# Recurrent gates on four 64x64 tiles, GpSimd subtractions in pieces, and a reordered prelude

## The chip, the cores and the metric

The kernel runs on one core of one Trainium2 chip. The core has TensorE (PE; PEld is its weight load), VectorE (DVE), ScalarE (ACT), GpSimd (POOL) and SyncE (SP), which issues nearly all DMAs from one queue in program order. The metric is the device time of one execution in microseconds. The kernel before took 1122.44 us (median of 3 runs, 1121.16 to 1125.28).

## The reference

One layer over 256 latent tokens and 256 context tokens, D = 1024, all in float32. Cut to its steps:

```python
mod = silu(c) @ w_ada + b_ada                     # 6 x 1024, also for c_ctx
zl  = modulate(rms_norm(x),   sh1, sc1) @ w_in    # 2048 columns
zc  = modulate(rms_norm(ctx), csh1, csc1) @ w_in  # only the recurrent columns count
conv_l = conformer_conv(zl[:, :512], zl[:, 512:1024])      # GLU, 31 taps, layer norm, silu
ul, uc = dwconv(zl[:, 1024:1536]), dwconv(zc[:, 1024:1536]) # 4 taps
for d in (forward, backward):                     # two directions
    r = sigmoid(u @ wa[d, head] + ba[d])          # 8 heads of 64 x 64
    i = sigmoid(u @ wx[d, head] + bx[d])
    a = exp(-8 r softplus(-lam[d]));  b = sqrt(1 - a^2) i u
    h += scan(a, b, start = end of the context's scan)
lru_l = h * gelu(zl[:, 1536:])
x = x + g1 * (concat(conv_l, lru_l) @ w_out)
h2 = modulate(rms_norm(x), sh2, sc2)
x = x + g2 * moe(h2)          # 32 experts of 1024 x 1024 x 3 weights, 2 per token
out = rms_norm(x)
```

## The kernel before

The **prelude** is everything ahead of the experts. Its weights (w_ada, w_in, w_out) pass through 17 slots of 128x2048 float32, the activations of the two token sets lie side by side as 512 columns. The **experts** follow one after another: each reads 12.6 MB of weights into nine 128x4096 buffers, wide0 to wide8, which lie on the memory of the prelude's slots and are used in the order of WORDER. So a weight load of the first round waits on SyncE's queue until the last prelude step that uses the memory under its buffer is done, and all later loads stand behind it. After expert 1 VectorE computes the largest expert load; SyncE reads it into a register (line 1038) ahead of the next loads on its queue.

**Split products.** Some float32 products are made from three fp32r passes. For that a weight is split: `split_hi` makes a rounded high half (HI, ZH, WH, MH name the engine by letters V, S, G), and `split_lo` (line 303) subtracts it to make the low half (LO, ZL, WL, ML). A slot has 2048 columns, so each is one instruction of 128x2048. `load_wz` and ZL do this for the four quarters of w_in's convolution columns, with `prepare` (lines 292 to 294) making the modulated inputs for `vgproj` (line 331); o0 and o1 do it for the recurrent columns u (used by `u_mm`, line 377), J4 for one part of w_out (used by `oproj`, line 680).

**Order.** From the end of the third quarter on, the prelude runs by the words of ORDER, a list written out by hand. Each word appends one step to the queues of its engines, which run in that order. The words that matter here: v vgproj, h and o the halves of u, l GLU, t a convolution tap on VectorE, s a side tap (scaled on ScalarE, added on GpSimd), i the same scaled on VectorE, u and c the recurrent projection and its 4 taps, p gate matmuls (`gate_mm`, line 397), a gate activations (`gate_act`, lines 407 to 414), d, q and n the recurrence, b one of 16 ada steps with its load (lines 505 to 511), z and e the gelu branch, M, C, Q, R and N the layer norm, I, J and X the splits for w_out, O the output projection, D, Y, H and K the second norm and router matmuls, T, P, F and A the selection, G and U the first gather, W idle matmuls (`warm`). With OS = "0010" only I4, J4, X4 and X5 do anything among the I, J and X words.

**Gates.** A gate step makes two banks, pa for r and pi for i. Each bank has the two heads of a 128-channel tile as 64x64 matmuls at tile positions (0, 0) and (64, 64). A float32 matmul stands in the trace as two records. `gate_act` takes three activations from pa, a square, and one tanh of pi with the halved biases hb (line 225).

Of the kernel before, what the change touches and what calls it, by code (L numbers as in the profile page):

```python
# [7 lines left out]
F32 = mybir.dt.float32  # L8
# [3 lines left out]
AF = mybir.ActivationFunctionType  # L12
OP = mybir.AluOpType
# [8 lines left out]
SLOTS = 17  # L22
WIDE = 9

WORDER = (0, 7, 5, 2, 1, 6, 4, 3, 8)


SP = 384
# [2 lines left out]


ORDER = """
v0 h0 o0 l0 v2 t v3 t h1 v1 t o1 u0 t*4 l2 u1 l1 t b t s b s t*2 s*2 t s t*2 s*2 t i t*2 s t l3 s*2 i t s t*4 s b t*2
s t c1 t*2 s*3 t s*2 t*2 s*2 t s i t c0 b*2 s u2 s*2 t p10 c2 s t s t p11 t s p00 b s a10 t a00 t i*2 u3 w b t*2 p20 t
i t*2 p01 s*2 c3 t p30 s*2 t*2 s t d10 s*2 i p21 t a20 s*2 t*2 d00 t a30 t d30 s t b t b z0 t s t a01 r1 d20 s q10 s*2
t*2 b t*2 s L0 t*2 s q20 t*4 L4 z1 I0 s q30 t p31 q00 t n00 t*2 n20 s b d01 a11 M b a31 k1 C2 z2 C1 a21 n10 C0 L2 d11
C3 d21 q11 b q21 q01 d31 z3 Q n01 b R e0 N1 N2 X1 N0 I2 L6 x b X2 N3 X0 n30 J2 J0 O001 e3 q31 O112 I4 e2 X3 n11 I6
O012 O111 O010 J4 b e1 O002 O100 O011 O110 g O113 n31 O102 n21 m1 X5 j J6 m3 O101 O000 O003 X7 O103 m0 O005 O017 O007
O013 r2 m2 X6 k2 X4 O006 O105 O104 O004 O015 O114 O014 D00 O107 O016 O115 D01 H00 O106 Y0 D10 O117 O116 H01 H10 y D11  # L40
K00 H11 K01 K10 Z0 T0 K11 P0 F0 G06 B G04 G02 Y1 T1 G07 G05 P1 Z1 G03 G00 F1 A1 G01 G10 G11 G12 U0 G16 G17 G14 G15 U4
U1 G13 U2 U3 U6 U5 U7 A0
"""
VTAPS = (31, 0, 9, 31)

PC = (0, 3)
SIDE = (1, 2,)
HI, LO = "SS", "GG"
SQ = ("SGGG", "SSSS")
LNSQ = "SGSG"  # L50
XC = ("VS", "SV")
WH, WL = "SSVV", "VVGV"
MH, ML = "GGGGGSSG", "GVGVGVGG"
GL = ("GG", "GG")
OS = "0010"
ZH, ZL = "SSSS", "GGGG"
FN = "VS"


COLS = {}  # L60
# [9 lines left out]
def hybrid_layer(ctx: ExitStack, tc: tile.TileContext, sp_d, x_d, c_d, bada_d, rb_d, fg_d, gw_d,  # L70
                 wada_d, win_d, wout_d, w1_d, w3_d, w2_d, out_d):
    nc = tc.nc
    V, S, G, P = nc.vector, nc.scalar, nc.gpsimd, nc.tensor
    dma = nc.sync.dma_start

    const = ctx.enter_context(tc.tile_pool(name="const", bufs=1))
# [33 lines left out]
    def col(name, i=None, n=1):  # L110
        a, b = COLS[name]
        return sp[:, a:b] if i is None else sp[:, a + i:a + i + n]
# [110 lines left out]
    V.tensor_scalar(nkh, kh, -1.0, None, OP.mult)  # L223
    hb = sp[:, COLS["ba"][0]:COLS["bx"][1]]
    V.tensor_scalar(hb, hb, 0.5, None, OP.mult)
    dwh = col("dw")
    V.tensor_scalar(dwh, dwh, 0.5, None, OP.mult)

# [54 lines left out]
    def f(a):  # L283
        return a.bitcast(F32)
# [15 lines left out]
            en.tensor_copy(hi, w)  # L300

    def split_lo(w, hi, lo, en):
        en.tensor_tensor(lo, w, f(hi), OP.subtract)  # L303


    def load_win(c0, i):
# [34 lines left out]
    w = load_wz(0)  # L341
# [3 lines left out]
    for q in range(4):  # L345
        ks = range(2 * q, 2 * q + 2)
        if q < 3:
            w = load_wz(q + 1)
# [9 lines left out]
    for i in range(2):  # L358
        w, hi, lo = slot(), slot_r(), slot_r()
# [3 lines left out]
    gw = slot()[:, 0:1024].rearrange("p (n m) -> p n m", n=16)  # L363
    dma(gw.rearrange("p n m -> p (n m)"), gw_d)
    uc_s = slot().rearrange("p (c t) -> p c t", c=4)
# [23 lines left out]

    lru, pgt, tgt = {}, {}, {}  # L390

    def gate_mm(ct, d):
        pa, pi = pgt[ct, d] = bank(), bank()
        for n, ps in enumerate((pa, pi)):
            for h in range(2):
                q = slice(64 * h, 64 * h + 64)
                P.matmul(ps[q, :], gw[q, d * 8 + n * 4 + ct], uc_s[q, ct], start=True, stop=True,
                         tile_position=(64 * h, 64 * h))

    def gate_act(ct, d, sq):  # L400
        if d not in lru:
            lru[d] = [slot().rearrange("p (c t) -> p c t", c=4) for _ in range(3)]
        va, vv, vw = lru[d]
        q = d * 4 + ct
        pa, pi = pgt.pop((ct, d))
        tr, a, a2, ti = t512(), va[:, ct], vv[:, ct], vw[:, ct]
        S.activation(tr, pa, AF.Tanh, scale=0.5, bias=hb[:, q:q + 1])
        S.activation(a, tr, AF.Exp, scale=nkh[:, q:q + 1], bias=nkh[:, q:q + 1])
        S.activation(tr, tr, AF.Tanh, scale=kh[:, q:q + 1], bias=kh[:, q:q + 1])
        if sq is S:  # L410
            S.activation(a2, a, AF.Square)
        else:
            sq.tensor_tensor(a2, a, a, OP.mult)
        S.activation(ti, pi, AF.Tanh, scale=0.5, bias=hb[:, 8 + q:9 + q])
        tgt[ct, d] = tr


# [404 lines left out]
    def route(t):  # L822
        val["r", t] = topk(t)

    steps = dict(v=lambda ct: vgproj(ct, (6, 7)), l=glu, t=vtap, s=stap, i=lambda: stap(True), u=u_mm, c=u_conv, p=gate_mm,
                 a=lambda ct, d: gate_act(ct, d, engines[SQ[d][ct]]), d=gate_v, q=root, n=scan, b=ada_step,
                 h=lambda i: split_hi(*wu[i], engines[HI[i]]), o=lambda i: split_lo(*wu[i], engines[LO[i]]),
                 w=load_wl, z=gelu_mm, e=gelu_act, m=lru_out, M=ln_mean,
                 C=lambda ct: ln_sub(ct, engines[LNSQ[ct]]), Q=ln_var, R=ln_rows, N=ln_out, r=row, k=cols,
                 g=g1_rows, B=quads, I=wo_hi, J=wo_lo, X=mixt_split, Z=first_split, y=second, x=router_row, j=router_rows, L=load_wo, O=oproj, W=warm,  # L830
# [3 lines left out]
    for word in ORDER.split():  # L834
        word, _, n = word.partition("*")
# [13 lines left out]
    def wide():  # L849
        n = WORDER[turn[0] % WIDE]  # L850
        turn[0] += 1
# [117 lines left out]
    for e in range(E - 1):  # L969
# [51 lines left out]
        for h in range(2):  # L1021
            o = (e % 2) * 64
# [80 lines left out]
    for f2 in range(2):  # L1103
        w = piece(2048).rearrange("p (k n) -> p k n", k=2)
# [49 lines left out]
    for w in TAIL.split():  # L1154
        i = int(w[1])
# [69 lines left out]
```

## Time and profile before

| | |
|---|---|
| median of 3 runs | 1122.44 us |
| profiled execution | 1124.29 us |
| its span | 1122.5 us |
| PE busy | 1001.9 us (89%) |
| DVE busy | 308.7 us (27%) |
| ACT busy | 173.7 us (15%) |
| POOL busy | 104.1 us (9%) |
| moved by DMA | 445.21 MB, mean 397 GB/s |

The shares are means over two very different parts. In the prelude (to about 198 us) all engines are busy and the DMA engines have gaps; in the experts the loads run at 430 GB/s nearly without one, and VectorE, ScalarE and GpSimd have little to do. An instruction that is held by another engine still counts as busy, so a long one among short ones of its kind is worth a look. A bracket behind a row of the timeline tells the idle time before it and what ended that.

### The profile page before, as it was taken

The numbers are of one execution on the slowest core, as the hardware profiler recorded it, in microseconds if no ns is written. First come the engines' busy times: TensorE is split into PE (matmuls) and PEld (weight loads), VectorE is DVE, ScalarE is ACT, GpSimd is POOL, SyncE is SP. The second block draws the span as 40 slices with busy tenths as digits, with TensorE's granted clock in tenths as the row PEclk, the third lists the DMA queues.
The fourth block names the chain that finished last, engine by engine and source line by source line (L and its number), as shares of the span: only waits on it lengthen the run. The fifth ranks groups of instructions, "written<-read, shape, count | busy, mean of one in ns | idle before, by whom it ended". The sixth has DMA issues, their size and how long they took to land.

```text
span 1122.5 us, 11836 instructions
## 1 busy us (share of the span) xinstructions
PE 1001.9 (89%) x4947; PEld 447.2 (40%) x4947; DVE 308.7 (27%) x625; ACT 173.7 (15%) x329; POOL 104.1 (9%) x107
## 2 busy tenths in 40 slices
PE   7889999999999999888888998988898989898795
PEld 6764547343434333323333333333333333232244
DVE  4788975221121112111211121112121111111113
ACT  3457944100000000000000000000000000000002
POOL 2487443000000000000000000000000000000001
PEclk9899997999999999999999999999999999999999
DMA  9756759989999999999999999999999999999994
GB/s 362 266 227 267 295 214 409 391 371 411 431 430 431 430 431 430 430 431 431 429 431 430 431 432 430 430 431 430 430 431 430 430 431 430 431 431 430 431 410 184
DMA packets 50015, 445.21 MB, mean 397 GB/s; under 512 B 4083, under 2 KB 14371, under 8 KB 24100
## 3 DMA queue, kind: packets, MB, share of 16 engines
q1 hardware_dynamic: 49746, 443.84, 94.2%
q8 instruction: 41, 0.67, 0.2%
q10 hardware_dynamic: 210, 0.55, 0.1%
q14 instruction: 18, 0.15, 0.0%
HBM read 443.32 MB, written 1.05 MB: 396 GB/s over the span
## 4 chain that ended last, share of the span: by engine, by line
DMA 57%; PE 33%; DVE 5%; POOL 1%; issue 1%; ACT 1%; SPq 1%; DVEq 0%; POOLq 0%; ACTq 0%
DMA wide<-in_w_dram 57%; PE bank L877 18%; PE bank L789 3%; PE bank L680 2%; PE bank L899 2%; PE bank L377 2%; PE bank L331 1%; PE bank L511 1%; DVE bank L469 1%; PE bank L815 1%; PE bank L315 1%; DVE slot L293 1%; PE bank L1004 1%; POOL slot L303 1%; SPq L1059 1%
## 5 line engine op out<-in xcount | busy, mean ns | idle before, releaser
L877 PE MATMUL bank<-wide,xg 128*64 128x512 f32 x1984 | 448.4, 596 | 78.6 <-DMA wide<-in_w_dram 78.5
L877 PEld LDWEIGHTS bank<-wide,xg 128*64 128x64 f32 x1984 | 141.4, 137 | 370.1 <-issue 256.7
L877 PE MATMUL bank<-wide,gt 128*64 128x512 f32 x992 | 219.9, 595 | 2.9 <-DMA wide<-in_w_dram 2.3
L987 DVE TENSOR_TENSOR sl<-sl,bank 128x512 f32<-128x512 f32 x31 | 21.3, 687 | 467.4 <-issue 443.8
L877 PEld LDWEIGHTS bank<-wide,gt 128*64 128x64 f32 x992 | 68.6, 137 | 141.8 <-issue 137.4
L1023 DVE TENSOR_TENSOR yy<-bank,g2bc 64x512 f32<-64x512 f32 x62 | 42.7, 688 | 193.4 <-PE bank L877 193.0
L1142 POOL TENSOR_TENSOR xg<-x,fgbc 128x256 f32<-128x256 f32 x6 | 4.2, 728 | 914.1 <-DMA wide<-in_w_dram 912.8
L980 ACT ACTIVATE sl<-bank 128x512 f32<-128x512 f32 x31 | 18.5, 597 | 437.5 <-PE bank L877 437.5
L789 PE MATMUL bank<-oh,xn 128*128 128x256 f32 x224 | 61.1, 416 | 0.0
L789 PEld LDWEIGHTS bank<-oh,xn 128*128 128x128 f32 x224 | 54.4, 327 | 11.4 <-issue 11.4
L899 PE MATMUL bank<-yy,st 128*128 128x512 f32 x120 | 58.0, 606 | 0.0
L1007 ACT COPY gt<-bank 128x256 f32<-128x256 f32 x31 | 11.6, 373 | 219.4 <-DVE gt L1006 219.4
L904 DVE TENSOR_TENSOR x<-x,bank 128x512 f32<-128x512 f32 x60 | 39.7, 683 | 7.1 <-PE bank L899 7.1
L795 ACT ACTIVATE xg<-bank,gsp 128x256 f32<-128x256 f32 x32 | 17.9, 564 | 153.7 <-PE bank L789 149.2
L303 POOL TENSOR_TENSOR slot<-slot 128x2048 fp32r<-128x2048 f32 x7 | 32.3, 4627 | 34.1 <-ACT slot L298 24.9
L331 PE MATMUL bank<-slot 128*128 128x256 f32 x192 | 28.7, 309 | 7.6 <-ACT slot L292 6.4
L899 PEld LDWEIGHTS bank<-yy,st 128*128 128x128 f32 x120 | 20.6, 191 | 26.5 <-issue 23.2
L331 PEld LDWEIGHTS bank<-slot 128*128 128x128 f32 x192 | 26.5, 211 | 9.7 <-ACT slot L292 7.4
L798 DVE TENSOR_SCALAR xg<-bank,gsp 128x256 f32<-128x256 f32 x32 | 17.2, 543 | 47.3 <-ACT xg L795 47.2
L377 PE MATMUL bank<-slot 128*128 128x512 f32 x96 | 22.9, 394 | 1.5 <-POOL slot L303 1.5
L1004 PEld LDWEIGHTS bank<-ident,sl 128*128 128x128 f32 x124 | 19.5, 204 | 11.1 <-issue 7.1
L487 POOL TENSOR_TENSOR xn<-xn,fgbc 128x256 f32<-128x256 f32 x30 | 22.5, 750 | 2.3
(249 smaller groups left out, 690.1 us busy)
## 6 DMA issues: line engine op xcount, KB each, us to landing
wide<-in_w_dram SPq DMA_DIRECT2D x186, 2048.0 KB, 38.7
slot<-in_wada_dram SPq DMA_DIRECT2D x16, 1024.0 KB, 6.2
slot<-in_wada_dram SPq DMA_DIRECT2D x16, 512.0 KB, 8.8
slot<-in_win_dram SPq DMA_DIRECT2D x8, 1024.0 KB, 9.1
wide<-in_w_dram SPq DMA_DIRECT2D x8, 1024.0 KB, 22.6
slot<-in_wout_dram SPq DMA_DIRECT2D x4, 1024.0 KB, 8.7
wide<-in_w_dram SPq DMA_DIRECT2D x8, 512.0 KB, 11.8
x<-in_x_dram SPq DMA_DIRECT2D x2, 512.0 KB, 4.4
```

The costliest lines, as they stand in the source:

```text
L303: en.tensor_tensor(lo, w, f(hi), OP.subtract)
L331: P.matmul(pvg[ct][:, i * T:(i + 1) * T], wz[k // 2][wi][:, k % 2, c:c + 128], x[k // 4][:, k % 4, 0:T], start=k + i + n == 0, stop=k == 7 ...
L377: P.matmul(pu, w, x[k // 4][:, k % 4], start=k + n == 0, stop=k == 7 and n == 2)
L487: G.tensor_tensor(acc, acc, p, OP.add)
L680: P.matmul(p, m[:, q], w[:, c:c + 512], start=first and n == 0, stop=len(done) == 8 and n == len(passes) - 1)
L789: P.matmul(pg[:, i * 256:(i + 1) * 256], xn[:, t, quad(k)], oh[:, t].rearrange("p e s -> p (e s)"), start=t + i == 0, stop=t == 1 and i == ...
L877: P.matmul(ps[64 * h:64 * h + 64, :], xs(k4 * 4 + i), w[:, i, h * 512:(h + 1) * 512], start=k4 + i == 0, stop=k4 * 4 + i == 7, tile_positi ...
L899: P.matmul(pz, st[:, t * 128:(t + 1) * 128], yy[:, h * 512:(h + 1) * 512], start=True, stop=True)
L904: V.tensor_tensor(x1[:, t, q], x1[:, t, q], pz, OP.add)
L987: V.tensor_tensor(gg, sl, pb, OP.mult)
L1004: P.transpose(pt[:, j * 128:(j + 1) * 128], gg[:, quad(j)], ident)
L1023: V.tensor_tensor(yy[o:o + 64, h * 512:(h + 1) * 512], py[64 * h:64 * h + 64, :], g2bc[64 * h:64 * h + 64, h * 512:(h + 1) * 512], OP.mult)
```

## The change

- The second bank of a gate takes its two heads at tile positions (0, 64) and (64, 0), so its output halves are swapped. Its tanh becomes two ScalarE instructions of 64 partitions, each from one half of the partitions to the other, with biases from a new tile hbx, which GpSimd copies with the halves swapped.
- `split_lo` on GpSimd works in pieces of LOPIECE = 512 columns.
- The second low half of u (LO) and that of w_out (WL, third letter) go from GpSimd to VectorE. Some squares, copies and high halves change engines (SQ, LNSQ, XC, MH). Letters of WH, WL, MH and ML at places where OS is 0 do nothing.
- ORDER is rearranged: among others an ada step now stands before u0, u1 behind l3, the gate steps are spread differently, J4 follows n11, four side taps change from s to i (s 46 to 42, i 7 to 11), and a W6 (six idle matmuls of 128 columns) stands between K10 and K11.
- WORDER, the order of the wide buffers, changes in its third to eighth places.

```diff
--- before.py
+++ after.py
@@ -22,7 +22,7 @@
 SLOTS = 17
 WIDE = 9
 
-WORDER = (0, 7, 5, 2, 1, 6, 4, 3, 8)
+WORDER = (0, 7, 2, 1, 4, 6, 3, 5, 8)
 
 
 SP = 384
@@ -31,30 +31,31 @@
 
 
 ORDER = """
-v0 h0 o0 l0 v2 t v3 t h1 v1 t o1 u0 t*4 l2 u1 l1 t b t s b s t*2 s*2 t s t*2 s*2 t i t*2 s t l3 s*2 i t s t*4 s b t*2
-s t c1 t*2 s*3 t s*2 t*2 s*2 t s i t c0 b*2 s u2 s*2 t p10 c2 s t s t p11 t s p00 b s a10 t a00 t i*2 u3 w b t*2 p20 t
-i t*2 p01 s*2 c3 t p30 s*2 t*2 s t d10 s*2 i p21 t a20 s*2 t*2 d00 t a30 t d30 s t b t b z0 t s t a01 r1 d20 s q10 s*2
-t*2 b t*2 s L0 t*2 s q20 t*4 L4 z1 I0 s q30 t p31 q00 t n00 t*2 n20 s b d01 a11 M b a31 k1 C2 z2 C1 a21 n10 C0 L2 d11
-C3 d21 q11 b q21 q01 d31 z3 Q n01 b R e0 N1 N2 X1 N0 I2 L6 x b X2 N3 X0 n30 J2 J0 O001 e3 q31 O112 I4 e2 X3 n11 I6
-O012 O111 O010 J4 b e1 O002 O100 O011 O110 g O113 n31 O102 n21 m1 X5 j J6 m3 O101 O000 O003 X7 O103 m0 O005 O017 O007
-O013 r2 m2 X6 k2 X4 O006 O105 O104 O004 O015 O114 O014 D00 O107 O016 O115 D01 H00 O106 Y0 D10 O117 O116 H01 H10 y D11
-K00 H11 K01 K10 Z0 T0 K11 P0 F0 G06 B G04 G02 Y1 T1 G07 G05 P1 Z1 G03 G00 F1 A1 G01 G10 G11 G12 U0 G16 G17 G14 G15 U4
-U1 G13 U2 U3 U6 U5 U7 A0
+h0 v0 o0 l0 v2 v3 t h1 t v1 t o1 b u0 t l1 l2 t s t*2 b s*2 t b s t*2 s t*5 s*2 t*2 l3 t*2 s*4 u1 s t*2 s t i t i t*2
+s t s c1 t*2 s*2 t s t u2 t c0 t*2 s*2 b s*3 b s p10 c2 s t i s t*2 p00 p11 s i t i t b a00 i t u3 w t a10 t*3 p20 t*2
+s i c3 p30 s b i t i t*2 d10 a20 s i t*2 a30 p01 t d00 s t*2 s b t s t b z0 t s t d20 d30 s r1 t*2 s b t a01 s z1 q10
+s*2 t*2 L0 t p21 t s L4 t q30 I0 q20 q00 s t*2 s t*3 p31 t n20 b i n00 d01 a11 M C1 a31 C2 k1 z2 a21 L2 d11 C0 C3 n10
+d21 q01 b d31 q11 q21 z3 Q n01 b R N1 N2 x X1 N0 b I2 L6 J2 X2 N3 J0 X0 e0 b O001 n30 e3 q31 I4 O111 O100 O011 X3 n11
+b J4 I6 O012 O002 O010 e2 O112 e1 g O113 m1 n31 m3 O000 O101 n21 X5 j J6 O110 O102 X7 m2 O103 X6 O017 O007 m0 O107
+O013 O005 O015 O003 r2 k2 X4 O104 O006 O105 O014 O004 O114 O016 D00 O115 D01 O106 D10 O116 H00 O117 Y0 H01 y D11 K00
+H10 H11 K01 K10 W6 Z0 K11 T0 P0 F0 G06 B G04 G02 Y1 T1 G05 G07 G03 P1 Z1 F1 G00 A1 G01 G12 G10 G11 G16 G14 G17 U0 G15
+U1 U4 G13 U2 U6 U5 U3 U7 A0
 """
 VTAPS = (31, 0, 9, 31)
 
 PC = (0, 3)
 SIDE = (1, 2,)
-HI, LO = "SS", "GG"
-SQ = ("SGGG", "SSSS")
-LNSQ = "SGSG"
-XC = ("VS", "SV")
-WH, WL = "SSVV", "VVGV"
-MH, ML = "GGGGGSSG", "GVGVGVGG"
+HI, LO = "SS", "GV"
+SQ = ("GGGG", "SSSS")
+LNSQ = "VGGS"
+XC = ("SS", "VV")
+WH, WL = "SSVS", "VGVG"
+MH, ML = "VSGGSSSG", "GVGGGVGG"
 GL = ("GG", "GG")
 OS = "0010"
 ZH, ZL = "SSSS", "GGGG"
 FN = "VS"
+LOPIECE = 512
 
 
 COLS = {}
@@ -223,6 +224,9 @@
     V.tensor_scalar(nkh, kh, -1.0, None, OP.mult)
     hb = sp[:, COLS["ba"][0]:COLS["bx"][1]]
     V.tensor_scalar(hb, hb, 0.5, None, OP.mult)
+    hbx = const.tile([128, 8], F32, name="hbx")
+    for h in range(2):
+        G.tensor_copy(hbx[64 * h:64 * h + 64], hb[64 - 64 * h:128 - 64 * h, 8:16])
     dwh = col("dw")
     V.tensor_scalar(dwh, dwh, 0.5, None, OP.mult)
 
@@ -300,7 +304,11 @@
             en.tensor_copy(hi, w)
 
     def split_lo(w, hi, lo, en):
-        en.tensor_tensor(lo, w, f(hi), OP.subtract)
+
+        n = w.shape[-1]
+        m = min(n, LOPIECE) if en is G else n
+        for c in range(0, n, m):
+            en.tensor_tensor(lo[:, c:c + m], w[:, c:c + m], f(hi)[:, c:c + m], OP.subtract)
 
 
     def load_win(c0, i):
@@ -389,13 +397,14 @@
 
     lru, pgt, tgt = {}, {}, {}
 
+
     def gate_mm(ct, d):
         pa, pi = pgt[ct, d] = bank(), bank()
         for n, ps in enumerate((pa, pi)):
             for h in range(2):
-                q = slice(64 * h, 64 * h + 64)
-                P.matmul(ps[q, :], gw[q, d * 8 + n * 4 + ct], uc_s[q, ct], start=True, stop=True,
-                         tile_position=(64 * h, 64 * h))
+                q, o = 64 * h, 64 * (h ^ n)
+                P.matmul(ps[o:o + 64, :], gw[q:q + 64, d * 8 + n * 4 + ct], uc_s[q:q + 64, ct], start=True, stop=True,
+                         tile_position=(q, o))
 
     def gate_act(ct, d, sq):
         if d not in lru:
@@ -411,7 +420,9 @@
             S.activation(a2, a, AF.Square)
         else:
             sq.tensor_tensor(a2, a, a, OP.mult)
-        S.activation(ti, pi, AF.Tanh, scale=0.5, bias=hb[:, 8 + q:9 + q])
+        for h in range(2):
+            o, i = slice(64 * h, 64 * h + 64), slice(64 - 64 * h, 128 - 64 * h)
+            S.activation(ti[o], pi[i], AF.Tanh, scale=0.5, bias=hbx[i, q:q + 1])
         tgt[ct, d] = tr
```

## Rows read from the trace of the kernel before

**Rows 1.** The chain that ended last, share of the span by engine (the page).
```profile
DMA 57%; PE 33%; DVE 5%; POOL 1%; issue 1%; ACT 1%; SPq 1%; DVEq 0%; POOLq 0%; ACTq 0%
```

**Rows 2.** SyncE's queue in order of time: start us, us, engine, line, what.
```profile
155.40 78.19 SPq L874 DMA_DIRECT2D wide<-in_w_dram  x18
...
251.77 0.31 SPq L1040 DMA_DIRECT2D fgbc<-in_fg_dram  x1
```

**Rows 3.** Windows: length, busy us of PE, PEld, DVE, ACT, POOL, clock, DMA share, GB/s.
```profile
155.40:245.00 89.60, 85.57 (x396) 46.30 (x396) 33.54 (x84) 20.95 (x45) 14.35 (x19) 0.92 0.97 404
245.00:255.00 10.00, 8.18 (x39) 2.58 (x37) 2.91 (x9) 0.00 (x0) 0.00 (x0) 1.00 0.55 212
255.00:1070.00 815.00, 733.17 (x3194) 280.02 (x3192) 138.05 (x262) 47.56 (x100) 0.00 (x0) 1.00 1.01 431
```

**Rows 4.** Whom SyncE's queue waited for: us in all, times, longest.
```profile
SPq L874 <- POOL slot L303: 13.7, 1, 13.7
...
SPq L1038 <- DVE so L885: 17.7, 1, 17.7
```

**Rows 5.** Order of time, around the first weight load.
```profile
150.52 4.86 POOL L303 TENSOR_TENSOR slot<-slot 128x2048 fp32r<-128x2048 f32 x1 [5.85 <-issue]
...
151.02 5.44 DVE L434 TENSOR_TENSOR_SCAN slot<-slot 128x512 f32<-128x512 f32 x1
```

**Rows 6.** Order of time, the first 62 us; in brackets idle time before, and its releaser.
```profile
24.30 4.51 POOL L303 TENSOR_TENSOR slot<-slot 128x2048 fp32r<-128x2048 f32 x1 [8.30 <-ACT slot L298]
24.47 4.37 DVE L218 TENSOR_SCALAR lw<-lw 128x8 f32<-128x8 f32 x1
...
30.05 0.17 DVE L225 TENSOR_SCALAR sp<-sp 128x16 f32<-128x16 f32 x1
...
31.78 0.80 PE L331 MATMUL bank<-slot 128*128 128x256 f32 x2 [4.71 <-ACT slot L292]
...
54.14 4.46 DVE L273 SCALAR_TENSOR_TENSOR g1s<-mod_a,sp 128x2 f32<-128x2 f32 x2
...
59.22 0.50 PE L331 MATMUL bank<-slot 128*128 128x256 f32 x2 [1.01 <-ACT slot L292]
```

**Rows 7.** Order of time, two 512-wide subtractions in the routing.
```profile
183.31 2.49 POOL L303 TENSOR_TENSOR t<-xn,t 128x512 fp32r<-128x512 f32 x2 [2.98 <-ACT t L781]
...
184.65 1.21 DVE L736 TENSOR_TENSOR pen<-pen,lg 128x32 f32<-128x32 f32 x1
```

**Rows 8.** Order of time, where the u projection goes on.
```profile
71.77 8.00 PE L377 MATMUL bank<-slot 128*128 128x512 f32 x34 [1.54 <-POOL slot L303]
```

**Rows 9.** Groups of instructions: shapes, count, busy us, mean ns, idle before.
```profile
L294 DVE TENSOR_TENSOR slot<-slot 128x256 fp32r<-128x256 f32 x16 | 6.8, 425 | 0.6
...
L987 DVE TENSOR_TENSOR sl<-sl,bank 128x512 f32<-128x512 f32 x31 | 21.3, 687 | 467.4 <-issue 443.8 <-PE bank L877 23.6
...
L1023 DVE TENSOR_TENSOR yy<-bank,g2bc 64x512 f32<-64x512 f32 x62 | 42.7, 688 | 193.4 <-PE bank L877 193.0
```

**Rows 10.** TensorE in order of time: ada steps, gates, one gate bank alone.
```profile
81.15 4.50 PE L511 MATMUL bank<-slot,silc 128*32 128x512 f32 x40
...
91.24 5.37 PE L397 MATMUL bank<-slot 64*64 64x512 f32 x24
...
112.65 1.07 PE L397 MATMUL bank<-slot 64*64 64x512 f32 x4 [1.19 <-ACT slot L414]
```

**Rows 11.** Windows of the middle of the prelude, and the gate's tanh by shape.
```profile
63.00:130.00 67.00, 62.06 (x347) 35.91 (x345) 57.90 (x105) 51.95 (x93) 51.94 (x57) 1.00 0.72 274
120.00:125.00 5.00, 5.00 (x27) 3.43 (x26) 4.72 (x11) 4.97 (x10) 4.48 (x6) 1.00 0.89 337
...
L414 ACT ACTIVATE slot<-bank,sp 128x512 f32<-128x512 f32 x8 | 5.3, 667 | 0.0
```

**Rows 12.** Windows and TensorE in order of time, the routing.
```profile
190.00:195.00 5.00, 5.00 (x32) 4.98 (x26) 2.21 (x11) 4.49 (x9) 2.69 (x2) 0.50 0.99 419
...
192.82 5.42 PE L815 MATMUL bank<-oh,t 128*128 128x256 f32 x22
```

## Prediction

> **What bounds the kernel now.** I read the chain that ended last first: 57% of the span is the load of the expert weights [rows 1], so the loads set the end, and the prelude sets when they can run. The DMA windows say by how much. From the first weight load at 155.40 us [rows 2] the DMA engines stay full but for one place: the share is 0.97 before it and 1.01 behind it, and 0.55 over the 10 us from 245, which leaves 4.5 us empty [rows 3]. There SyncE's queue stood still for 17.7 us, because it loads a register that VectorE writes after expert 1 [rows 4], and issued again at 251.77 us [rows 2]. So two moments set the end: when expert 1 is done on TensorE (call the gain there g2) and when the first weight load may start (g1). The end comes earlier by the smaller of g2 and g1 + 4.5. The first weight load waits on GpSimd's long subtraction [rows 4], which runs until 155.38 us [rows 5]. Everything before that is the prelude, and there I read, stretch by stretch, what TensorE waits for.
>
> **GpSimd's low halves in short pieces, and the new bias copy.** A 2048-wide subtraction on GpSimd takes 4.5 us, and the VectorE instruction that starts inside it ends with it: 4.37 us for an 8-column operation, 4.46 us for two of 2 columns [rows 6]. Operations as small take 0.17 us beside it (the one at 30.05, [rows 6]), so some 4.2 us are lost each time, on the way to the scales that ScalarE and then TensorE need. There are four such stalls, one to a quarter. TensorE's own idle time is what can be won: 4.71 us at 31.78 and 1.01 us at 59.22 [rows 6], with smaller ones behind them about 7.5 us.
>
> The change adds a wait: the copies into hbx read VectorE's halved biases (made at 30.05 us, [rows 6]) and stand on GpSimd's queue ahead of the first subtraction, which ran from 24.30. Behind it wait the third pass of vgproj(0) and the weight slots that SyncE refills. At first the wait helps: VectorE is no longer held, has its biases at about 30.05 - 4.2 = 25.9 us, and TensorE can begin 3 to 4 us earlier. GpSimd's pieces then run from about 26.3 to 31.6 us and collide with the next chain of VectorE instructions. What that costs is seen in two 512-wide subtractions that take 2.49 us together: the second stretched a 32-column VectorE instruction to 1.21 us [rows 7]. That is one hold per piece, so four pieces can hold a dependent chain by 4 x 1.25 = 5.0 us: pieces help the instruction that comes first, and only where it is the urgent one. The scales of a quarter are such (two instructions, so one or two pieces instead of four). Bounds: 1 us (only the last stall shrinks) and 7.5; I take 4.5, nearest to the two stalls at which TensorE was idle, since it was busy under the other two.
>
> The Trainium skill (SBUF — State Buffer, section "SBUF: two separate sides") says that the ports shared by these engines are an exclusive lock: whoever starts first has them for the whole instruction. The rows above show just that; by the rule alone a chain of small operations gains nothing from pieces, which is a rival below.
>
> **The second low half of the u weights moves to VectorE (LO "GV").** GpSimd did both in sequence, and TensorE stood idle 1.54 us for the second [rows 8]. VectorE needs about 2.2 us for it: 0.425 us for 256 columns and 0.687 for 512 are 0.26 per further 256 [rows 9], so 0.687 + 6 x 0.26. An ada step now stands before u0 as cover. Its load is on the same SyncE queue, where the ada, w_in and w_out loads keep their number and shift by a few places. Gain 1.5 us, bounds 0 and 1.5.
>
> **Gates on four tiles.** Now 24 records of 64x64 take 5.37 us, 0.447 us per two [rows 10]: two tiles run at once, and all 64 records cost some 15 us with what stands between. Four column tiles do run at once in the ada steps: 40 records in 4.50 us, 0.45 per four [rows 10]. If the four 64x64 tiles do so too, TensorE is freed of some 7 us. But TensorE isn't the last there: single banks run alone after 1.19 us of idle time behind ScalarE's gate activation [rows 10], and ScalarE is busy 4.97 of 5 us [rows 11]. The swapped halves cost ScalarE one more tanh for each of 8 gates. No row has a ScalarE operation of this size on 64 partitions; VectorE's takes 688 ns on 64 and 687 on 128 [rows 9], so I take the full 0.667 us [rows 11]: +5.3 us (2.7 if half the partitions took half the time). Off ScalarE go a square and the scaling of four side taps, which become VectorE's (i steps 7 to 11, s steps 46 to 42); at about 0.5 us each that is 2.5, so net +2.8 us on the engine that paces this stretch. Against it: GpSimd is free 4.5 us sooner for its taps, and a gate has both banks after one pass. I take +1 us, bounds -3 (the added ScalarE work all on the path) and +5 (TensorE's 7 us but for what ScalarE takes back).
>
> The Trainium skill (TensorEngine Tiling (Array Packing), section "PSUM Bottleneck") warns that tiling doesn't speed up the emptying of PSUM; the ScalarE row agrees, and by it the gain here would be none. Its section "Gotcha 1: PSUM Pressure" says that different row tiles cannot access one bank at the same time; the pairs of 0.447 us share a bank, so the trace differs.
>
> **Layer norm and output projection.** The last square moves from GpSimd to ScalarE; at GpSimd's rate (4.86 us for 2048 columns, [rows 5]) that is 0.6 us, and TensorE has other matmuls beside it: +0.5, bounds 0 and 0.6. The low half of w_out moves from GpSimd to VectorE, behind scan n11. GpSimd's 4.86 us stretched a VectorE scan to 5.44 us [rows 5]; VectorE pays 2.2 us and gets that hold back, so the step would end a little earlier within the projection than now, and g1 follows the prelude's gain, near 8. The load order (WORDER) follows the slots that come free; I cost it at nothing, hidden behind the 4.5 us of slack, and at what exceeds that if wrong. The other engine letters swap operations of 256 columns: nothing.
>
> **Idle passes (W6).** They are 12 records of 128 columns, by the 512-column pace of 0.45 [rows 10] about 0.11 us each, 1.3 us. The granted clock is 0.50, the lower level of 1.2 GHz, in 190 to 195 us, after TensorE had only narrow router matmuls, and the 22 gather records from 192.82 take 5.42 us [rows 12]; at the upper level half, so 2.7 us to win, and under 1 in the shorter ones before. But the passes stand at about 183 us, and TensorE idles again behind them for the selection on VectorE. They delay K11 by 1.3 us, which that selection hides. Bounds -1 and +3.5; I take +1.
>
> **The sum.** 4.5 + 1.5 + 1 + 0.5 + 1 = 8.5 us for g2; g1 + 4.5 is over 12, so g2 counts. The profiled execution took 1124.29 us (span 1122.50), 1.85 over the median 1122.44: 1124.29 - 8.5 = 1115.8, in terms of the median 1114. Its own range by likely errors of the terms is 1109 to 1118.
>
> **Rivals.**
> - *More of it works* (the clock stays up, VectorE and ScalarE keep pace with the shorter gates): 7 + 1.5 + 4.5 + 0.5 + 2.5 = 16 us, 1106 us. For it: ScalarE has 15 us and VectorE 9 us of idle time in the 67 us from 63 [rows 11]. Against: little of it lies where ScalarE is full.
> - *Early gain eaten*: the 6 us of the first stretch arrive at ScalarE, which pays 2.8 net back and waits where it did before: about 3 us remain, 1119.5 us.
> - *Four tiles don't overlap, or pieces hold VectorE as long as before* (one hold per piece, rows 7): 4 to 5 us less in either case, 1118 to 1119 us.
> - *Slower: VectorE becomes the bound.* It is given 2.2 + 2.2 + about 2 = 6.4 us, and ScalarE 2.8 more to feed it, in a stretch in which it is busy 57.9 of 67 us [rows 11]. If its idle time is spent on waits for ScalarE and can't be used, the projection starts 9.2 us later. It decides as soon as pieces and bias copy give the first stretch under 3.6 us (9.2 less the 5.6 that can be told); with nothing from there and 3.5 from the other terms it is 1122.4 + 9.2 - 3.5 = about 1128 us. Against it: two long subtractions fewer collide with VectorE.
>
> **How the numbers follow.** Forecast 0.48, more of it 0.17, early gain eaten 0.15, tiles or pieces without effect 0.10, slower 0.10. A measurement of this kernel tells about 0.5% from no change, 5.6 us, so faster is below 1116.8: nearly all of the forecast (0.44), the first rival, and 0.01 of the others: 0.62. Slower is 0.10, the rest, 0.28, the same. The range reaches from inside the first rival to the unchanged time: 1105 to 1122.
>
> **What would show it.** In the changed profile: VectorE instructions held for no more than about 1.3 us before 62 us; TensorE starting vgproj near 28 us, and u0 without idle time; a gate's eight records in about 1.1 us; two 64-partition tanh per gate and ScalarE full over a longer stretch; the first weight load near 147 us; the register load still between the weight loads, near 243. The prediction is wrong if the halves of tanh stretch the gates, if SyncE's queue waits on a slot that now comes free later, or if the clock of the routing shows 1.00 and the gathers halve.

## The result, and the profile after

The changed kernel took 1132.72 us (median of 4 runs, 1131.94 to 1134.44) against 1123.86 for the kernel before: a ratio of 1.0085 [1.0068, 1.0102], so 0.85% slower where 0.8% faster was forecast. The profiled execution took 1132.48 us with a span of 1130.6.

The chain that ended last in the changed kernel, share of the span by engine (answers [rows 1]), has the same shape as before:

```profile
DMA 58%; PE 32%; DVE 6%; ACT 1%; SPq 1%; issue 1%; POOL 0%; DVEq 0%; ACTq 0%
```

SyncE's queue in order of time (answers [rows 2]):

```profile
153.71 79.77 SPq L885 DMA_DIRECT2D wide<-in_w_dram  x18
251.61 0.31 SPq L1051 DMA_DIRECT2D fgbc<-in_fg_dram  x1
```

In these two profiles both moments on which the forecast rested stand where they stood: g1 is 1.7 us, g2 is 0.16. So no gain arrived, but no loss either up to 252 us. (The two profiles begin at different clocks; the section on experiments comes back to this.) Windows of the changed kernel (answers [rows 3]; the columns are as there):

```profile
153.71:245.00 91.29, 86.88 (x413) 46.46 (x413) 31.47 (x82) 21.27 (x46) 12.19 (x18) 0.94 0.95 397
245.00:255.00 10.00, 8.18 (x41) 2.61 (x39) 2.91 (x9) 0.00 (x0) 0.00 (x0) 1.00 0.57 212
255.00:1070.00 815.00, 731.67 (x3170) 278.72 (x3168) 138.05 (x262) 47.57 (x100) 0.00 (x0) 1.00 1.01 427
```

The last line is the loss: the DMA engines are as full as before (1.01), and move 427 GB/s instead of 431. It sits where the diff edits nothing, in the weight loads. Their packets of 16 KB, between 289 and 989 us of the span, took (ns: how many, the commonest)

```
before   mean 612.1    611: 18315   612: 13
after    mean 616.9    614: 10215   621: 3972   613: 1701   619: 1131   612: 1129
```

616.9 / 612.1 is 1.0078, and over the some 930 us from the first to the last of these packets that is 7.3 us, most of what was lost.

What differs for the loads is where they land. In the program's memory plan wide0 starts at byte 66048 of a partition in the kernel before (a multiple of 512) and at 66080 in the changed one: the new tile hbx, 8 float32 in a partition, is 32 bytes among the constants, and everything behind it moves up by these. The other eight buffers follow wide0 at steps of 16384 bytes, so all nine are off by 32.

The prelude did change inside. VectorE, GpSimd and TensorE in order of time (answers [rows 6]):

```profile
25.02 5.17 POOL L311 TENSOR_TENSOR slot<-slot 128x512 fp32r<-128x512 f32 x4
25.10 1.27 DVE L277 SCALAR_TENSOR_TENSOR g1s<-mod_a,sp 128x2 f32<-128x2 f32 x2
27.69 1.37 DVE L298 TENSOR_TENSOR slot<-slot 128x256 fp32r<-128x256 f32 x1
28.98 1.35 DVE L297 TENSOR_SCALAR slot<-slot,g1s,mod_a 128x256 f32<-128x256 f32 x1
...
32.48 4.55 PE L339 MATMUL bank<-slot 128*128 128x256 f32 x36
...
50.10 10.69 POOL L311 TENSOR_TENSOR slot<-slot 128x512 fp32r<-128x512 f32 x8 [3.66 <-ACT slot L302]
51.58 1.40 DVE L298 TENSOR_TENSOR slot<-slot 128x256 fp32r<-128x256 f32 x1
52.90 1.38 DVE L297 TENSOR_SCALAR slot<-slot,g1s,mod_a 128x256 f32<-128x256 f32 x1
...
58.42 6.75 PE L339 MATMUL bank<-slot 128*128 128x256 f32 x42 [3.75 <-DVE slot L298]
...
62.94 2.28 DVE L311 TENSOR_TENSOR slot<-slot 128x2048 fp32r<-128x2048 f32 x1
...
67.55 4.83 PE L385 MATMUL bank<-slot 128*128 128x512 f32 x20
```

The copies into hbx hold GpSimd back as foreseen, and the scales are there at 26.4 us. But from 27.69 on each VectorE instruction that meets a piece is held for it: 1.3 to 1.4 us instead of 0.4. In the last quarter GpSimd runs eight pieces in one row, and the dependent chain of VectorE pays each of them, from 51.58 to 61 us; TensorE then stands idle for 3.75 us. What was won at 32.48 us (35.78 before, but 34.09 in before_w6, a run of the old prelude that begins at the same clock as this profile) is given back by 65.17, the end of vgproj (66.99 before, 65.30 in before_w6).

TensorE in the gates, and ScalarE's tanh by shape (answers [rows 10] and [rows 11]):

```profile
88.07 2.79 PE L406 MATMUL bank<-slot 64*64 64x512 f32 x20
92.29 1.08 PE L406 MATMUL bank<-slot 64*64 64x512 f32 x4 [1.43 <-DVE slot L394]
99.96 1.09 PE L406 MATMUL bank<-slot 64*64 64x512 f32 x8
104.15 1.09 PE L406 MATMUL bank<-slot 64*64 64x512 f32 x8 [3.10 <-DVE slot L394]
125.77 1.97 PE L406 MATMUL bank<-slot 64*64 64x512 f32 x4 [4.91 <-DVE xn L480]
```

```profile
L425 ACT ACTIVATE slot<-bank,hbx 64x512 f32<-64x512 f32 x12 | 8.2, 684 | 0.2
```

```profile
63.00:130.00 67.00, 57.56 (x332) 33.01 (x331) 61.56 (x109) 51.77 (x90) 45.43 (x56) 0.95 0.68 269
```

Four tiles do run at once (20 records in 2.79 us; 24 took 5.37 before), and a tanh on half the partitions takes as long as one on all. TensorE's work falls by 4.5 us, from 62.06 to 57.56; VectorE's rises by 3.7, to 61.56 of 67 us, and it is now VectorE for which TensorE waits.

### The profile page after: what moved, and what is told of

It is laid out like the page before. It is cut to its first block, busy times and chain, and to the rows that moved or that the text cites. A ratio compares the mean times of both kernels' runs of the same rounds, so it can differ in the third digit from the quotient of the medians.

```text
span 1130.6 us, 11884 instructions
## 1 busy us (share of the span) xinstructions
PE 1002.3 (89%) x4959; PEld 445.6 (39%) x4959; DVE 312.8 (28%) x632; ACT 177.1 (16%) x331; POOL 97.8 (9%) x122
## 4 chain that ended last, share of the span: by engine, by line
DMA 58%; PE 32%; DVE 6%; ACT 1%; SPq 1%; issue 1%; POOL 0%; DVEq 0%; ACTq 0%
DMA wide<-in_w_dram 57%; PE bank L888 17%; PE bank L800 3%; PE bank L691 2%; PE bank L910 2%; DVE bank L480 1%; PE bank L339 1%; PE bank L385 1%; PE bank L522 1%; DVE slot L394 1%; DMA slot<-in_wada_dram 1%; PE bank L826 1%; PE bank L323 1%; PE bank L1015 1%; DVE xn L480 1%; DVE slot L298 1%
## 5 line engine op out<-in xcount | busy, mean ns | idle before, releaser
L311 POOL TENSOR_TENSOR slot<-slot 128x512 fp32r<-128x512 f32 x20 | 26.5, 1358 | 9.3 <-ACT slot L302 9.3
```

Source lines behind the costliest of these rows:

```text
L311: en.tensor_tensor(lo[:, c:c + m], w[:, c:c + m], f(hi)[:, c:c + m], OP.subtract)
```

## Experiments

Ratios are against runs of the kernel before on the same chip, with the 95% interval.

**Where the wide buffers start.** First the shift alone, in the kernel before:

```diff
     V.tensor_scalar(hb, hb, 0.5, None, OP.mult)
+    pad = const.tile([128, 8], F32, name="pad")
+    V.memset(pad, 0.0)
```

> The kernel before with one unused 128x8 float32 tile (32 bytes per partition) among the constants, and nothing else, so that every tile allocated later, the wide buffers among them, starts 32 bytes further on (wide0 at 66080 bytes instead of 66048). Placement theory: each 16 KB packet of the weight loads takes about 617 ns instead of 611, the stretch behind 255 us runs at 427 GB/s instead of 431, and the time is 1131 to 1133 us. Rival, order of the buffers (or the reordered prelude itself): packets at 611 ns and about 1123 us, as the kernel before.

1133.46 us, 1.0093 [1.0059, 1.0127]. 32 unused bytes reproduce the whole loss, with packets at 616.9 ns. Its window of the experts:

```profile
255.00:1070.00 815.00, 728.22 (x3166) 277.80 (x3164) 138.13 (x262) 47.56 (x100) 0.00 (x0) 1.00 1.01 427
```

Next the other thing that touches the loads, their order, exchanged both ways (the line of the one kernel in the other; here the change's order undone):

```diff
-WORDER = (0, 7, 2, 1, 4, 6, 3, 5, 8)
+WORDER = (0, 7, 5, 2, 1, 6, 4, 3, 8)
```

> The changed kernel with the buffer order WORDER of the kernel before; the 32 bytes of hbx stay. Placement theory: packets stay at 617 ns, 1131 to 1135 us (a little worse than the changed kernel if a slot comes free later in this order). Rival, order of the buffers sets the rate: 611 ns and 1123 to 1125 us.

> The kernel before with the buffer order WORDER of the changed kernel, no other edit. Placement theory: packets stay at 611 ns; 1122 to 1127 us, the upper end if the third buffer of this order comes free later in the old prelude. Rival, order of the buffers sets the rate: 617 ns, 1131 us or more.

1135.66 us, 1.0114 [1.0082, 1.0146], with packets at 616.9 ns; and 1123.24, 0.9993 [0.9979, 1.0006], with 612.1. The order of the buffers does nothing to the rate.

How far must a buffer be moved for the loss to go? With hbx 64 bytes wide:

```diff
-    hbx = const.tile([128, 8], F32, name="hbx")
+    hbx = const.tile([128, 16], F32, name="hbx")[:, 0:8]
```

> The changed kernel with the tile hbx made 16 columns wide instead of 8 (64 bytes instead of 32; the second half is unused), so wide0 starts at 66112, a multiple of 64. Placement theory: packets back to 611 ns, 431 GB/s, and 1123 to 1124 us, since the first expert and the register load come within 0.3 us of the kernel before. Rival, order of the buffers: 1132 us as the changed kernel.

1133.49 us, 1.0085 [1.0056, 1.0115], 616.0 ns: 64 bytes are not enough, and my expectation was wrong. Then nine different starts in the kernel before, by small tiles between the wide buffers:

```diff
     for n in range(WIDE):
+        if n:
+            wx.tile([128, 8 if n < 5 else 16], F32, name=f"space{n}")
         wx.tile([128, 4096], F32, name=f"wide{n}")
```

> The kernel before with unused spacers between the nine wide buffers, so that wide0 to wide8 start 0, 32, 64, 96, 128, 192, 256, 320 and 384 bytes past a multiple of 512. One profile gives the packet time of each buffer. If 128 bytes of alignment suffice: 611 ns for wide0, wide4, wide6 and wide8, 614 to 621 for the others. If 256: wide0 and wide6 alone. If 512: wide0 alone. If the loss isn't a matter of the single buffer's start but of the whole layout: all buffers alike. Time between 1126 and 1133 us.

1129.32 us, a mean packet of 614.5 ns. The trace doesn't name a packet's buffer; with the packets put to the loads in order of time, 128 to a load, the means by buffer are about 612 ns at an offset of 0, 617 at 32, 615 at 64, 96 and 192, 611 at 128, 613 at 256 and 320, and 615 to 616 at 384. That is no clean curve, and none of the patterns that I had expected. Loads of neighbouring buffers are under way together, which may blur it. So I moved all nine alike, by a tile ahead of wide0:

```diff
+    wx.tile([128, 32], F32, name="space")    # 128 bytes; 64: 256 bytes, 128: 512 bytes
     for n in range(WIDE):
         wx.tile([128, 4096], F32, name=f"wide{n}")
```

> The kernel before with 128 bytes in front of the first wide buffer, so that all nine start at 128 modulo 512. Theory (a start that is a multiple of 128 bytes is as good as one of 512): a 16 KB packet takes 611 ns, 431 GB/s, 1121 to 1125 us. Rival (it must be a multiple of 512): 613 to 617 ns, 427 to 429 GB/s, 1128 to 1134 us.

> 256 bytes in front of the first wide buffer: all nine start at 256 modulo 512. Theory (only a multiple of 512 bytes is free of it): packets of 16 KB at 613 to 617 ns on the mean, 427 to 429 GB/s. Rival (256 is enough): 611 to 612 ns, 431 GB/s. The time is no measure here, since the moved buffers wait for other tiles of the prelude than before.

> 512 bytes in front of the first wide buffer, so that each lies elsewhere but on a multiple of 512 again. Theory (it is the multiple that counts): 611 to 612 ns, 431 GB/s. Rival (it is the place itself, or that the buffers were moved at all): 613 to 617 ns, 427 to 429 GB/s. The time is no measure here, as for 256.

The times, 1139.5, 1135.7 and 1138.31 us, say nothing on the rate, since the moved buffers lie on tiles that are in use for longer: at 128 bytes SyncE's queue stood for up to 33.8 us at one weight load. For the first my expectation of the time was therefore wrong on both sides. The rate is read from the packets, and they are clear:

```
offset of all nine   0 (before)   32     64     128    256    512
mean packet, ns      612.1        616.9  616.0  615.9  612.1  612.0
GB/s, 255 to 1070    431          427    427    428    431    431
```

The figures at 32 are those of the changed kernel, at 64 those with the wider hbx. A multiple of 256 bytes is free of the loss, 128 isn't. That the buffer at 128 read 611 ns among unlike neighbours stays unexplained.

**The change with its buffers in place.** hbx moves to a pool behind the constants, and wide0 is back at 66048:

```diff
-    hbx = const.tile([128, 8], F32, name="hbx")
+    hbx = big.tile([128, 8], F32, name="hbx")
```

> The changed kernel with the tile hbx in the pool that lies behind the wide buffers (big) instead of among the constants ahead of them, so wide0 is back at 66048 bytes; nothing else is changed. Placement theory: packets 611 ns, 431 GB/s, and 1122 to 1125 us, because the first expert starts only 0.3 us earlier than in the kernel before and the register load 0.2 us. Rival 1, the reordered prelude loses time by itself: over 1127 us. Rival 2, the prelude's gain was there and hidden by the slow loads: 1114 to 1119 us.

1126.58 us, 1.0037 [1.002, 1.0054], packets at 612.1 ns. That is between the theory's range and the first rival's. Of the 8.9 us some 5.4 are gone and 3.4 remain (2 to 6 by the interval); the packets are back at their old rate, so the rest is lost elsewhere, by the profiles below ahead of the experts. (The same 32 bytes added 9.5 us to the kernel before; 7.3 is what the packets give. Executions of the kernel before spread over some 8 us, and a chip's few runs don't settle such a difference.) The next two start from this kernel. First whole subtractions:

```diff
-LOPIECE = 512
+LOPIECE = 2048
```

> As after_big, with LOPIECE = 2048, so GpSimd's low halves are single instructions again. Theory (pieces hold every VectorE instruction of a dependent chain for one piece of 1.3 us, and help only the first): the first matmuls of the last quarter of the convolution projection, idle for 3.75 us in the changed kernel, start within 1 us of there, and the time is within 2 us of after_big. Rival, the pieces carry the early gain: 3 to 5 us slower than after_big, first expert 3 us later.

then, in pieces again, two tiles to a gate with one tanh:

```diff
-                P.matmul(ps[o:o + 64, :], gw[q:q + 64, d * 8 + n * 4 + ct], uc_s[q:q + 64, ct], start=True, stop=True,
-                         tile_position=(q, o))
+                P.matmul(ps[q, :], gw[q, d * 8 + n * 4 + ct], uc_s[q, ct], start=True, stop=True,
+                         tile_position=(64 * h, 64 * h))
...
-            S.activation(ti[o], pi[i], AF.Tanh, scale=0.5, bias=hbx[i, q:q + 1])
+        S.activation(ti, pi, AF.Tanh, scale=0.5, bias=hb[:, 8 + q:9 + q])
```

> As after_big, with the gate matmuls at two tile positions and one tanh for the second gate, as in the kernel before. Theory (VectorE paces 81 to 125 us and TensorE waits for it): TensorE is busy some 4 to 7 us longer between 88 and 130 us and idle that much less, ScalarE has 5 us less work, and the time is the same within 2 us, or faster by up to 3. Rival, four tiles are worth what they free on TensorE: 4 to 7 us slower than after_big.

Whole subtractions: 1125.27 us, 1.0028 [1.0016, 1.004]; the pieces gain nothing, if anything they cost 1 us. Two tiles: 1130.53 us, 1.0067 [1.0052, 1.0082]; in the new order the four tiles are worth 4 us, which I had not expected.

A warning on reading single profiles here: executions begin at different clocks. The granted clock of the first 16 us was 0.89 in nine of the twenty profiles, 1.00 in nine others, 0.95 and 0.79 in one each. It was 0.89 in the profile of before and 1.00 in that of after, and the first expert comes about 2 us later with the lower one, the kernel being the same or nearly so. At 1.00 the first expert starts at 196.11 us in before_w6 and 196.93 in before_gates, against 197.90 in after and 197.76 in big_whole; at 0.89 at 198.18 in before, against 200.62 in after_big. So "unchanged up to 252 us", as the two profiles had it, was the luck of the clock: at a like clock the new prelude is 1 to 2.4 us late.

It isn't late in the same place each time. In after and big_whole vgproj ends at 65.17 and 65.28 us, as in before_w6 (65.30), and the delay comes behind it. In after_big it ends at 69.74, against 66.99 in before, which is more than the whole delay of the first expert. There GpSimd's second four pieces follow the first four at once, VectorE's chain meets all eight, and TensorE idles twice (GpSimd and TensorE of after_big in order of time):

```profile
32.22 5.48 POOL L311 TENSOR_TENSOR slot<-slot 128x512 fp32r<-128x512 f32 x4 [0.22 <-ACT slot L302]
...
35.34 1.65 PE L339 MATMUL bank<-slot 128*128 128x256 f32 x6 [3.62 <-DVE slot L298]
...
62.94 6.79 PE L339 MATMUL bank<-slot 128*128 128x256 f32 x42 [3.69 <-DVE slot L298]
```

Against the old prelude at the same clock, after_worder (0.89) and big_two (1.00) are 2.6 to 2.8 us late at the end of vgproj too, and before_gates_w6 below (0.89, whole subtractions, the old order) 3.8 us. All four have the copies into hbx ahead of GpSimd's first subtraction, as have five profiles that are not late there; of the ten without them that begin at 0.89 to 1.00 none is late. So a part of what remains belongs to the bias copy and the pieces, in some executions; how often, one profile of each kernel doesn't tell.

**The parts one by one, in the kernel before.** The four tiles with their tanh (the last diff the other way round, with hbx in big), W6, and both:

```diff
-K00 H11 K01 K10 Z0 T0 K11
+K00 H11 K01 K10 W6 Z0 T0 K11
```

> The kernel before with the four-tile gates, the two 64-partition tanh and hbx alone; hbx lies behind the wide buffers, so these stay on a multiple of 512 bytes. Theory (in the order before, the gates hide beside VectorE's and ScalarE's work): the same within 2 us of the kernel before, 1121 to 1125 us. Rival (the 4 us that the gates are worth in the order after come from the tiles themselves): 1118 to 1120 us. Second rival (the eight more 64-partition tanh, 0.69 us each on ScalarE, cost more than the tiles save): 1125 to 1128 us.

> The kernel before with the idle passes W6 alone, at the place where the order after has them (ahead of Z0). Theory: the clock in the routing rises from 0.76 to near 1.00 in 180 to 185 us and the first expert comes 0.5 to 1.5 us earlier, 1121.5 to 1123 us. Rival (routing waits for VectorE, not for the clock): the same, 1123 us. Second rival (the passes stand in front of the router's products on TensorE): slower by up to 1.5 us, 1123.5 to 1125 us.

> Both of the last two in the kernel before. If the two act in different stretches, their differences add: 1119 to 1123 us. Rival (a stretch that ends earlier only moves the low clock to another place): no faster than the better of the two.

1124.54 us, 1.0017 [1.0005, 1.0029]; 1123.0, 1.0002 [0.999, 1.0015]; 1123.7, 1.0007 [0.9993, 1.002]. In the old order the tiles, with their tanh and hbx, are worth nothing and may cost 1 to 2 us, between the theory and the rival on ScalarE. In the profile of before_gates the chain that ended last lies on ScalarE for 26.7 of the 65 us from 66 to 131, in before_w6 for 0.8. W6 moves nothing: the gathers still take 5.44 us for 22 records (5.42 in [rows 12]). That it raises the clock isn't shown: over 180 to 205 us it is 0.86 in before_w6, but 0.80 in before_gates_w6, and 0.73 or 0.80 in the ten profiles of the old order without W6.

```profile
181.78 1.58 PE L154 MATMUL bank<-ones 128*128 128x128 f32 x12
...
185.51 0.41 PE L750 MATMUL bank<-msk,tri 128*128 128x32 f32 x2 [1.32 <-DVE msk L745]
186.75 0.71 PE L815 MATMUL bank<-oh,t 128*128 128x256 f32 x2 [0.83 <-DVE oh L770]
...
190.74 5.44 PE L815 MATMUL bank<-oh,t 128*128 128x256 f32 x22
```

(before_w6, TensorE in order of time.) Behind the passes TensorE waits twice for VectorE's selection, and the gathers run at the lower pace again, at a granted clock of 0.54 from 190 to 195 us.

What is left is the choice of engines and the order. Each goes into the kernel before alone, as it stands in the change's diff: the engine letters from HI, LO to MH, ML, of which these two lines show the kind, and then ORDER with nothing else.

```diff
-HI, LO = "SS", "GG"
+HI, LO = "SS", "GV"
...
-XC = ("VS", "SV")
+XC = ("SS", "VV")
```

> The kernel before with the change's choice of engines alone (o1's low half and the squares, splits and copies that change engine), in the order before. Theory (the 2 to 3 us that the change loses ahead of the first expert come from the new order, which was laid out for other engines): the same, 1121.5 to 1124.5 us, first expert 195 to 197 us where the clock of the first 16 us is 1.00, 197 to 199 where it is 0.89. Rival (VectorE and ScalarE, which bound the stretch from 82 to 126 us, get more work by it): 1125 to 1127 us, first expert 1.5 to 3 us later than that.

> The kernel before with the change's order of steps alone (W6 with it), two tiles to a gate and the engines of before. Theory: this is where the loss sits: 1125 to 1130 us, first expert 198 to 203 us at a clock of 1.00 in the first 16 us. Rival (the order costs nothing by itself): 1121.5 to 1124.5 us, first expert 195 to 197 us.

1123.09 us, 0.9998 [0.9985, 1.0012], and 1127.07, 1.0034 [1.0019, 1.0049]. The order by itself, with two tiles to a gate, costs some 3 us. That doesn't add up with the other parts: big_two, which has this order with the new engines, the pieces and hbx, is 7.4 us over the kernel before, and the four tiles take 4 of these back. What the engines and the pieces cost in the new order no run separates. Where before_order is late shows at the layer norm's sums over the convolution's output; before_order, in order of time:

```profile
128.31 0.33 DVE L484 TENSOR_SCALAR fgbc<-cb,sp 128x256 f32<-128x256 f32 x1
128.78 1.04 POOL L487 TENSOR_TENSOR g2bc<-g2bc,fgbc 128x256 f32<-128x256 f32 x1 [4.56 <-DVE fgbc L484]
129.90 0.99 POOL L489 TENSOR_TENSOR xn<-xn,g2bc 128x256 f32<-128x256 f32 x1
130.94 2.07 PE L577 MATMUL bank<-xn,ones 128*128 128x256 f32 x4 [2.79 <-POOL xn L489]
...
157.25 80.01 SPq L874 DMA_DIRECT2D wide<-in_w_dram  x18
255.40 0.31 SPq L1040 DMA_DIRECT2D fgbc<-in_fg_dram  x1
```

and the same in before_w6, which has the old order, the same W6 and the same clock (1.00) in its first 16 us:

```profile
127.71 0.48 DVE L469 SCALAR_TENSOR_TENSOR xn<-cb,sp,bank 128x256 f32<-128x256 f32 x1
128.25 1.99 PE L577 MATMUL bank<-xn,ones 128*128 128x256 f32 x8 [1.65 <-DVE xn L469]
...
153.69 77.83 SPq L874 DMA_DIRECT2D wide<-in_w_dram  x18
249.71 0.31 SPq L1040 DMA_DIRECT2D fgbc<-in_fg_dram  x1
```

In the old order VectorE ends the convolution at 128.19 us and TensorE goes on 0.06 us later. In the new one a VectorE scaling (an i step) stands behind two recurrent scans, and then two GpSimd additions follow: the sums end at 133.01 us against 130.24, 2.8 us later, the first weight load comes 3.6 us later, the register load 5.7 (what is added behind the sums I did not follow). In big_whole the sums stand behind the same i step and additions and end at 131.66, 1.4 us later than in before_w6.

What leads there is VectorE. The stretch from 82 to 104 us, in before_w6 and then in before_order (columns as in [rows 3]):

```profile
82.00:104.00 22.00, 22.00 (x116) 11.72 (x110) 18.05 (x32) 16.30 (x31) 16.68 (x23) 1.00 0.58 215
...
82.00:104.00 22.00, 20.49 (x101) 10.46 (x99) 21.29 (x36) 16.71 (x30) 15.79 (x21) 1.00 0.62 229
```

In the old order TensorE has no idle time there and VectorE 4 us; in the new one VectorE has 0.7 us left and TensorE waits. The chain that ended last, followed back from the sums, lies on TensorE up to 101.58 us in before_w6, with pieces such as the first two lines here, and in before_order on VectorE from 81.98 us to the two additions, but for one gate at 104.15, with pieces such as the third:

```profile
83.92 5.67 PE bank L377 x24
...
95.88 5.70 PE bank L377 x24
...
98.11 0.85 DVE xn L469
```

It does so in the changed kernel as well: 42.3 of the 65 us from 66 to 131 lie on VectorE in after and in big_whole, 19.7 in before and before_w6. VectorE's busy time over a longer stretch hides this. From 66 to 130 us it is 59.19 us in before_order and 55.28 in before_w6, but 59.49 in before_engines, where the sums, the first expert and the register load come within 0.3 us of before. There 4.2 us of it are o1's low half, which starts at 65.06; from 82 to 126 it is 40.74 us, against 42.55 in before_order. So the new order makes VectorE the engine that the prelude waits for in this stretch; that this is its whole loss isn't shown.

**The model of the end.** The prediction has the end follow the smaller of g2 and g1 + 4.5. To test the 4.5, the register load moves from expert 2 to expert 6:

```diff
-        if e == 2:
+        if e == 6:
             nmax = nc.values_load(fmi[0:1, 0:1], min_val=0, max_val=T)
-        if e == 2:
+        if e == 6:
             dma(fgbc[0:1, :], fg_d)
```

> The kernel before with the register load (and the small load behind it) after expert 6 instead of expert 2, so that SyncE's queue doesn't stand still for expert 1. Theory (as in the prediction: the DMA engines are empty for 4.5 us near 245 us, and the weight loads set the end): 4 to 4.5 us faster, 1118.5 to 1119.5 us, no window of 10 us under 400 GB/s behind 215 us. Rival (the hole only moves: the nine buffers are full and wait for TensorE, or the queue stands still at expert 6 instead): the same, 1122 to 1124 us.

> The same step in the changed kernel with its wide buffers in place and whole subtractions (big_whole). Theory (without the hole the first weight load sets the end, and that comes no later than in the kernel before): what expert 1 loses no longer counts, 1117.5 to 1120 us, level with before_reg6. Rival (the new order's 3 us stay): 3 us behind before_reg6.

1118.74 us, 0.9961 [0.9945, 0.9977]: the 4.5 us, as worked out, and a kernel that beats both. SyncE's queue and the window of the former hole in before_reg6:

```profile
155.37 171.54 SPq L874 DMA_DIRECT2D wide<-in_w_dram  x39
```

```profile
245.00:255.00 10.00, 8.18 (x39) 2.58 (x37) 2.91 (x9) 0.00 (x0) 0.00 (x0) 1.00 1.02 436
```

The queue no longer stands still, and the DMA share is 1.02 where it was 0.55 [rows 3]. The changed prelude with the same step took 1120.6 us, 0.9972 [0.9959, 0.9985]: 1.9 us behind by the medians, 1.2 by the ratios, whose intervals overlap. So the runs don't tell the two expectations apart, level or 3 us behind. Its profile, which begins at 1.00, has the first weight load at 153.13 us (153.69 in before_w6 at the same clock).

## Why the prediction was wrong

- **The step that failed** is the sum's silent premise that the weight loads keep their rate. I took hbx for a copy on GpSimd's queue and its wait, and WORDER for the only thing that touches the loads. That hbx also takes memory ahead of the buffers on which 57% of the span rests [rows 1], I did not see. No rival had it either: the one on the slower side, VectorE as the bound, came to 1128 us by another way. The price, 0.78% of the weight loads' some 930 us, could not be read from the trace of before; the question could have been asked. The Trainium skill (DMA: Bandwidth & Descriptors, section "How a descriptor splits into AXI transactions") says that a transfer is split at multiples of 256 bytes, and that a read which starts off such a multiple fetches the bytes ahead of its start too, at a cost. Here the side that moved is the one written, in SBUF. The runs agree on the 256; the size differs: an estimate by that page, carried over to writes, gives 513 beats of 32 bytes for 512 at an offset of 32 bytes, 0.2%, and 516 at 128, 0.8%, and the packets show 0.78% and 0.62%. Why the loss doesn't grow with the offset stays open.
- **Pieces and hbx, +4.5.** The rows that I read had the price: one hold per piece [rows 7]. The first scales came early, and of the 3.3 us at 32.48 that the two profiles show 1.6 are left at a like clock (34.09 in before_w6). Mis-sized was what follows: the pieces hold the 256-column chain as well, four or eight times, and at the end of vgproj 0.1 us is left at a like clock (65.17 against 65.30 in before_w6), or 2.8 us are lost (after_big, 69.74 against 66.99). Whole subtractions in big_whole end at 65.28. The rival "pieces hold VectorE as long as before" is what happened.
- **o1 to VectorE, +1.5.** The 2.28 us (2.2 estimated) and u0 without idle time came. But an ada step and other matmuls went ahead of u0, which starts at 67.55 us against 65.13 in before_w6; with all changed engines alone the time is the same.
- **Gates, +1 (-3 to +5).** The mechanism was right in each row: four tiles at once, 64 partitions at full price. The size depends on the order: -1.6 us in the old one (with hbx's copies), +4 in the new.
- **Layer norm and output projection, +0.5.** No run separates it.
- **W6, +1.** Nothing. Whatever the clock was ahead of the selection, behind it the gathers ran at the lower pace, as feared, and their 2.7 us did not come.
- **The order.** I priced the words that moved past each other, not the engine on which the longest path comes to lie. By itself it costs 3.1 us. The rival "VectorE becomes the bound" has the place and the engine right: TensorE waits for VectorE, at 125.77 us in the changed kernel among others, and the chain lies on VectorE. Its price of 9.2 us was too high: the sums end 1.4 us later in big_whole, 2.8 in before_order. And the changed engines, which it held to give VectorE most of its added work, do not bring it about alone (before_engines); the order does.
- **The end.** The 4.5 us of slack held: taking the hole away gave 4.5 us. The rest of the rule, the smaller of g2 and g1 + 4.5, was not put to a test, since neither gain came.

## What to carry to other kernels

When a change adds a tile, however small, look where the buffers land that lie behind it: if the loads set the time, keep their start on a multiple of 256 bytes, or put the new tile behind them. Read the hole in the loads first: moving one register load gave 4.5 us, and this rework of the prelude lost time. A prelude in which five engines hand work on is judged by the engine on which its longest path lies, stretch by stretch, not by what each engine has to do over the whole, and by profiles that start at the same clock.

## What the hardware showed that I had not expected

- 16 KB packets into SBUF took 612 ns on the mean with the start at a multiple of 256 bytes and 616 to 617 ns at 32, 64 and 128 bytes past one, with all 16 engines full. The loss doesn't grow with the offset.
- A GpSimd subtraction of 512 columns held one VectorE instruction beside it to 1.3 to 1.4 us, two of 2 columns together 1.27, one of 256 columns 1.40; eight of them in a row held eight.
- Four 64x64 tiles at positions (0, 0), (64, 64), (0, 64) and (64, 0) ran at once: eight records of 512 columns in 1.09 us, where pairs took 0.447 us per two.
- ScalarE's tanh of 512 columns took 684 ns on 64 partitions and 667 ns on 128.
